# Gate loads cut in six and bound to places in the SP queue, gate stores issued from ScalarE, a shorter last norm

## The chip, the cores and the metric

One Trainium2 chip, one core in use. The metric is the device time of one execution in microseconds (us). TensorE (PE) multiplies matrices, VectorE (DVE) and ScalarE (ACT) work on tiles, GpSimd (POOL) issues indirect loads here, SyncE (SP) only issues direct loads and stores. SP, ACT and POOL each have a queue of transfers; the transfers themselves run on 16 shared DMA engines.

## The reference, cut to what matters

One decoder layer over 512 tokens of width 1024, in float32: a conditioning step, a combined projection, two kinds of attention, an output projection and a layer norm give `x1`. What the change touches is the second half, a product-key expert layer (PEER) with 16384 experts:

```
q   = h @ w_pq ; scores against sub_keys ; top 16 per half, then top 16 of the 256 pairs -> idx, g = softmax
a   = gelu(u_tab[idx] . h)
ffn = sum over idx of (g * a) * v_tab[idx]
out = LayerNorm(alpha * x1 + gate2 * ffn) * ln2_g + ln2_b
```

## The kernel before

The tokens are four tiles of 128 (`NT`). Tile 0 and half of tile 1 (`HU` = 64 tokens) fetch their experts' rows one by one, by indirect loads on POOL's queue (`fetch`, L742; one transfer brings one 1024-wide row for each of 128 partitions), followed by a DVE operation for each: a dot product with `h` (L747) for `u_tab`, an accumulation into `acc0` (L783) for `v_tab`. All other tokens are computed densely, over all experts in 128 blocks of 128.

**The u stage** (`u_block`, 128 blocks, about 345 to 970 us). A block loads 512 KB of `u_tab` (`load_raw`, L93, three buffers), splits it into a rounded part `hi` (ACT, L87) and a remainder `lo` (DVE, L88; three buffers each), multiplies with 24 matmuls of 320 columns (L97 to L99) and applies Gelu (ACT, L815). Blocks 0 to 31 keep their activations on the chip, blocks 32 to 111 store them to `a_d` from ACT's queue (L820), blocks 112 to 127 keep them again. Beside the blocks run three generators: `topk` (DVE), `make_g` and the gathers. `make_g` builds the dense gate matrix of a tile of tokens in 16 steps (one-hot vectors on DVE, scaled by eight `go` operations on ACT, 16 matmuls, two copies to `stage` on ACT); after each two steps, 1 MB goes to `g_d` in device memory, issued on SP (L700). For three tiles that is 48 steps and 24 stores. Constants set the rate per block: `GRATE` steps of `make_g`, `RA`, `RB` and `RV` us worth of gathers (each 1.25 or 1.2), and a budget of 2.6, 1.6 or 0.7 us of `topk`.

**The v stage** (`v_block` and `v_mm`, 128 blocks, about 968 to 1527 us). A block loads 512 KB of `v_tab` (L93), splits it as above, multiplies the activations with the gates to `w` (L884 on ACT, L885 on DVE), splits `w` to `wh` and `wl` (L890, L891; four buffers) and does 18 matmuls of 512 columns. The gates come in groups of eight blocks (`GB`), 16 groups, each one load of 1.5 MB in runs of 512 bytes, issued on ACT (`g_load`, L863). There are two gate buffers: `gl`, and `gl2`, which takes over the place of the transposed activations that the u stage multiplies. From the 49th block on, each block also loads its activations back from `a_d` (L881, four buffers, on SP). At block 112 seven loads of 512 KB are written down for the end (`g2r`, `ln2g`, `ln2b`, four `xr`, L912 to L917). At block 116 all gathers that are left are pulled at once, and `finish(0)` normalizes tile 0. The last six blocks are multiplied tile by tile, each followed by `finish` of that tile.

**The order.** The code is written in program order, but a planner sorts the instructions of each queue while the kernel is built: an instruction whose inputs and buffers are free by the planner's own reckoning goes ahead of one that isn't, earlier-written ones first. On the chip each queue then keeps that order strictly, so an instruction that must wait holds up all those behind it in its queue. Waits are on buffers being free, on data, and for a transfer also on an earlier transfer that used the same one of a few completion counters.

```python
nc.scalar.dma_start(gl, g_d.rearrange("g p i t -> p g (i t)")[:, :, e * TG:(e + GB) * TG])
dma(a, a_d[e - NB])
dma(g_d[(t - 1) * (P // TG) + tg], stage)
```

Of the kernel before, what the change touches and what calls it, by code (L numbers as in the profile page):

```python
# [36 lines left out]
NB = 32  # L37
GB = 8
NS = 80
GRATE = 0.54  # L40
HU = 64
T0U = P + HU
TU = S - T0U
# [1 line left out]
GBUF = 5  # L45
RA = 1.6
RB = 1.9
RV = 1.45


@with_exitstack
def layer(ctx: ExitStack, tc: tile.TileContext, A, out, dbg=None):
# [31 lines left out]
    def split(src, shape, eng_hi=None):  # L84
# [3 lines left out]
        split.last = nc.vector.tensor_sub(lo, src, hi.bitcast(F32))  # L88
        return hi, lo

    def load_raw(src, shape):
        raw = stream.tile(shape, F32, name="raw", tag="raw", bufs=3)
        dma(raw, src)  # L93
        return raw

    def mm3(ps, lh, ll, rh, rl, first, last):
        nc.tensor.matmul(ps, lh, rh, start=first, stop=False)  # L97
# [7 lines left out]
        nc.gpsimd.tensor_tensor(r, v, mhalf.to_broadcast([P, n]), op=OP.pow)  # L105
        return r

    def normalize(pool, pre, half):
        st = pool.tile([P, 2, 6], F32, name="ln_st", tag="ln_st", bufs=2)
        for i in range(2):  # L110
            half(slice(i * 512, (i + 1) * 512), i)
            nc.vector.bn_stats(st[:, i, :], pre[:, i * 512:(i + 1) * 512])
        mv = pool.tile([P, 2], F32, name="ln_mv", tag="ln_mv", bufs=2)
        nc.vector.bn_aggr(mv, st)
        r = rsqrt_eps(pool, mv[:, 1:2], 1)
        nc.vector.tensor_scalar(pre, pre, mv[:, 0:1], r, op0=OP.subtract, op1=OP.mult)

    hh = hpool.tile([P, KB, S], F32R, name="hh", tag="hh")
# [549 lines left out]
    def make_g(t, pool):  # L668
        i01, g = best[t]
        ps = accbank()  # L670
        nc.tensor.transpose(ps[:, 0:P], i01[:, 0].rearrange("p h k -> p (h k)"), ident)
        nc.tensor.transpose(ps[:, P:2 * P], i01[:, 1].rearrange("p h k -> p (h k)"), ident)
        nc.tensor.transpose(ps[:, 2 * P:3 * P], g.rearrange("p h k -> p (h k)"), ident)
        iT = pool.tile([P, 3, P], F32, name="iT", tag="iT", bufs=1)
        nc.scalar.copy(iT.rearrange("p a t -> p (a t)"), ps[:, :3 * P])
        iTb = pool.tile([P, P], BF, name="iTb", tag="iTb", bufs=1)
        nc.scalar.copy(iTb, ps[:, :P])
        for tg in range(P // TG):
            stage = pool.tile([P, NKEY, TG], F32, name="stage", tag="stage", bufs=2)
            for q in range(TG // 8):  # L680
                t0 = tg * TG + q * 8
                oh0 = pool.tile([P, P, 8], BF, name="oh0", tag="oh0", bufs=2)
                nc.vector.tensor_tensor(oh0, iTb[:, None, t0:t0 + 8].to_broadcast([P, P, 8]), iota8, op=OP.is_equal)
                oh1 = pool.tile([P, 8, P], F32, name="oh1", tag="oh1", bufs=2)
                nc.vector.tensor_tensor(oh1, iT[:, 1, t0:t0 + 8, None].to_broadcast([P, 8, P]),
                                        iota[:, None, :].to_broadcast([P, 8, P]), op=OP.is_equal)
                go = pool.tile([P, 8, P], F32, name="go", tag="go", bufs=2)
                for i in range(8):
                    nc.scalar.activation(go[:, i, :], oh0[:, :, i], AF.Copy, scale=iT[:, 2, t0 + i:t0 + i + 1])  # L689
                for u in range(2):  # L690
                    ps = accbank()
                    for i in range(4):
                        nc.tensor.matmul(ps[:, i * P:(i + 1) * P], oh1[:, 4 * u + i, :], go[:, 4 * u + i, :],  # L693
                                         start=True, stop=True)
                    w = q * 8 + u * 4
                    nc.scalar.copy(
                        stage[:, :, w:w + 4].rearrange("p i t -> p t i"), ps.rearrange("p (t i) -> p t i", t=4))
                if q < TG // 8 - 1:
                    yield
            dma(g_d[(t - 1) * (P // TG) + tg], stage)  # L700
            yield

    best = {}
# [123 lines left out]
    c1 = c2 = 0.0  # L827
    gt = gathers()
    late = []
    for e in range(NKEY):  # L830
        if e == NB + NS:
            pull(tk, 1e9)
            while not weighted:
                next(gt)
            drain(gg)
            g_stack.close()
            sel_stack.close()
            late.append(ctx.enter_context(tc.tile_pool(name="late", bufs=1, reuse_waits="tile")))
        u_block(e)
        keep(e)  # L840
        if e < NB + NS:
            budget[0] = pull(tk, budget[0] + (2.6 if 1 not in best else 1.6 if 2 not in best else 0.7))
        if 2 in best and e < NB + NS:
            c1 += GRATE
            while c1 >= 1.0:
                c1 -= 1.0
                drain(gg, 1)
        if 1 in lists:
            c2 = pull(gt, c2 + (RA if not weighted else RB))
    psB_stack.close()  # L850
    psq[:] = ctx.enter_context(tc.tile_pool(name="psC", bufs=1, space=bass.MemoryType.PSUM, reuse_waits="tile")), 2, 6

    v_stack = ExitStack()
    vp = v_stack.enter_context(tc.tile_pool(name="vp", bufs=1, reuse_waits="tile"))
    pacc = [[accbank() for _ in range(2)] for _ in range(DT)]
    order = list(range(NB)) + list(range(NB + NS, NKEY)) + list(range(NB, NB + NS))

    def g_load(e):
        if e // GB % 2 == 0:
            gl = vp.tile([P, NTG, GB * TG], F32, name="gl", tag="gl", bufs=1)  # L860
        else:
            gl = hpool.tile([P, NTG, GB * TG], F32, name="gl2", tag="hh")
        nc.scalar.dma_start(gl, g_d.rearrange("g p i t -> p g (i t)")[:, :, e * TG:(e + GB) * TG])  # L863
        return gl

    gls = {order[0]: g_load(order[0])}

    def v_block(n):
        e = order[n]
        gl = gls[e - e % GB]  # L870
        raw = load_raw(A["v_blk"][e], [P, D])
        if n < NKEY - 4:
            hi, lo = split(raw, [P, D])
        else:
            hi, lo = (b[:, n - NKEY + 4, :] for b in tail[1:])
            nc.scalar.copy(hi, raw)
            nc.vector.tensor_sub(lo, raw, hi.bitcast(F32))
        a = acts.pop(e)
        if a is None:
            a = vp.tile([P, TU], F32, name="a_b", tag="a_b", bufs=4)  # L880
            dma(a, a_d[e - NB])  # L881
        w = vp.tile([P, TD], F32, name="w", tag="w", bufs=2)
        i = e % GB
        nc.scalar.copy(w[:, 0:HU].rearrange("p (g t) -> p g t", t=TG), gl[:, 0:HU // TG, i * TG:(i + 1) * TG])  # L884
        nc.vector.tensor_mul(w[:, HU:].rearrange("p (g t) -> p g t", t=TG), a.rearrange("p (g t) -> p g t", t=TG),  # L885
                             gl[:, HU // TG:, i * TG:(i + 1) * TG])
        wp, nb = (vp, 4) if n < NKEY - 3 else (tail[0], 3)
        wh = wp.tile([P, TD], F32R, name="wh", tag="wh", bufs=nb)
        wl = wp.tile([P, TD], F32R, name="wl", tag="wl", bufs=nb)
        nc.scalar.copy(wh, w)  # L890
        pace[0], pace_next[0] = pace_next[0], nc.vector.tensor_sub(wl, w, wh.bitcast(F32))  # L891
        return n, hi, lo, wh, wl
# [8 lines left out]
    tail = [None]  # L901
    last = []
    for n in range(NKEY):
        if n % GB == 0 and n + GB < NKEY:
            gls[order[n + GB]] = g_load(order[n + GB])
        c2 = pull(gt, c2 + RV)
        if n == NKEY - 16:
            ring_stack.close()
            fin = ctx.enter_context(tc.tile_pool(name="fin", bufs=1, side="right", reuse_waits="tile"))
            tail[0] = fin  # L910
            g2r, ln2g, ln2b = (fin.tile([P, D], F32, name=nm) for nm in ("g2r", "ln2g", "ln2b"))
            dma(g2r, g2_d[0].partition_broadcast(P))  # L912
            dma(ln2g, A["ln2_g"].partition_broadcast(P))
            dma(ln2b, A["ln2_b"].partition_broadcast(P))
            xr = [fin.tile([P, D], F32, name=f"xr{t}") for t in range(NT)]
            for t in range(NT):
                dma(xr[t], x1_d[t])  # L917
            pre = [h2n] + [fin.tile([P, D], F32, name=f"pre{t}") for t in range(DT)]
            hi4 = hpool.tile([P, 4, D], F32R, name="hi4", tag="hh")
            lo4 = hpool.tile([P, 4, D], F32R, name="lo4", tag="hl")  # L920
            tail += [hi4, lo4]
        if n == NKEY - 12:
            pull(gt, 1e9)

            def finish(t, src):
# [2 lines left out]
                    nc.vector.scalar_tensor_tensor(pre[t][:, s], xr[t][:, s], ALPHA, pre[t][:, s],  # L928
                                                   op0=OP.mult, op1=OP.add)

                normalize(vp, pre[t], half)
                for f in range(2):
                    fs = slice(f * 512, (f + 1) * 512)
                    nc.vector.tensor_mul(pre[t][:, fs], pre[t][:, fs], ln2g[:, fs])
                    nc.vector.tensor_add(pre[t][:, fs], pre[t][:, fs], ln2b[:, fs])
                    dma(out[t][:, fs], pre[t][:, fs])

            finish(0, (acc0[:, 0:512], acc0[:, 512:1024]))
        blk = v_block(n)
        if n < NKEY - LAST:  # L940
            for t in range(DT):
                v_mm(t, *blk)
        else:
            last.append(blk)
# [79 lines left out]
```

## Time and profile before

| | us |
|---|---|
| median of three runs | 1546.8 (1546.06 to 1556.96) |
| the profiled execution, time | 1547.63 |
| its span in the profile | 1545.7 |
| PE busy | 1430.1 (93%) |
| DVE busy | 1265.8 (82%) |
| ACT busy | 822.6 (53%) |
| POOL busy | 462.5 (30%) |
| mean granted clock of TensorE | 0.965 |
| moved by the DMA engines | 446.17 MB, 289 GB/s |

Busy time is what an engine spends in instructions; the issue of a transfer is not counted. A count behind an x is a number of instructions. "A <- B" in a list of waits means that A stood idle until B was done.

### The profile page before, as it was taken

How to read it: one execution, taken by the hardware profiler on the slowest of the kernel's cores; microseconds unless marked ns; L12 is line 12 of the kernel's file. 1: busy time of each engine (PE TensorE's matmuls, PEld its weight loads, DVE VectorE, ACT ScalarE, POOL GpSimd, SP SyncE). 2: the span in 40 equal slices, each digit the busy share in tenths (PEclk: the TensorE clock that was granted, in tenths of full speed). 3: DMA queues.
4: the chain of work that ended last, by engine and by line, in shares of the span. 5: the costliest groups of instructions: out<-in, count | busy, mean ns of one | idle time of the engine just before them, and what ended most of it. 6: DMA issues, size and time to landing. Idle time of an engine off the chain costs nothing.

```text
span 1545.7 us, 22766 instructions
## 1 busy us (share of the span) xinstructions
PE 1430.1 (93%) x7837; PEld 1254.9 (81%) x7837; DVE 1265.8 (82%) x2606; ACT 822.6 (53%) x1523; POOL 462.5 (30%) x338
## 2 busy tenths in 40 slices
PE   6999988998789998999999969899889999999985
PEld 5677866887789998999999969788768888888854
DVE  7797675899899899678798759688679788897896
ACT  2466533334358998999798734344234343433431
POOL 0000000000344333044354436334324444454420
PEclk9999898999899999999999989999989999999997
DMA  8856363222688899699899999999989999999971
GB/s 312 286 186 196 119 203 117 84 85 67 233 282 308 314 349 332 199 339 403 347 385 380 402 322 393 337 342 321 326 304 363 370 363 374 380 356 359 374 281 54
DMA packets 180245, 446.17 MB, mean 289 GB/s; under 512 B 15329, under 2 KB 86369, under 8 KB 176930
## 3 DMA queue, kind: packets, MB, share of 16 engines
q1 hardware_dynamic: 73122, 238.66, 43.2%
q0 software_dynamic: 46080, 167.79, 28.9%
q10 hardware_dynamic: 60928, 38.28, 8.2%
q8 instruction: 61, 1.00, 0.3%
q14 instruction: 54, 0.44, 0.1%
HBM read 401.38 MB, written 43.26 MB: 288 GB/s over the span
## 4 chain that ended last, share of the span: by engine, by line
PE 49%; DVE 15%; issue 11%; DMA 9%; ACT 9%; POOL 5%; POOLq 0%; DVEq 0%; ACTq 0%; SPq 0%
PE acc L97 9%; PE acc L98 9%; PE acc L99 8%; POOL gb L742 5%; PE bank L97 5%; PE bank L98 4%; PE bank L99 4%; ACT go L689 4%; DMA gl<-g_d 4%; DVE lo L88 3%; DMA raw<-v_blk 2%; ACT hi L87 2%; PE st L98 2%; PE st L97 2%; PE st L99 2%
## 5 line engine op out<-in xcount | busy, mean ns | idle before, releaser
L87 ACT CAST hi<-raw 128x1024 fp32r<-128x1024 f32 x286 | 299.3, 1050 | 298.8 <-PE acc L99 82.6
L88 DVE TENSOR_TENSOR lo<-raw,hi 128x1024 fp32r<-128x1024 f32 x286 | 349.4, 1222 | 124.7 <-ACT hi L87 123.8
L97 PE MATMUL st<-h2h,hi 128*128 128x320 f32 x1024 | 324.1, 317 | 20.4 <-ACT hi L87 20.4
L99 PE MATMUL st<-h2h,lo 128*128 128x320 f32 x1024 | 319.7, 313 | 15.9 <-DVE lo L88 15.7
L97 PE MATMUL acc<-hi,wh 128*128 128x512 f32 x768 | 302.6, 395 | 20.0 <-ACT hi L87 13.9
L98 PE MATMUL st<-h2l,hi 128*128 128x320 f32 x1024 | 319.5, 312 | 0.0
L98 PE MATMUL acc<-lo,wh 128*128 128x512 f32 x768 | 302.2, 394 | 1.7 <-DVE lo L88 1.7
L99 PE MATMUL acc<-hi,wl 128*128 128x512 f32 x768 | 300.7, 393 | 1.1 <-DVE wl L891 1.0
L742 POOL DMA_INDIRECT gb<-v_tab,ei x128 | 182.6, 1426 | 251.4 <-DVE acc L783 228.4
L742 POOL DMA_INDIRECT gb<-u_tab,ei x128 | 179.4, 1402 | 261.2 <-DVE gb L747 192.4
L747 DVE SCALAR_TENSOR_TENSOR gb<-gb,h2n 128x1024 f32<-128x1024 f32 x192 | 231.5, 1220 | 13.0 <-DMA gb<-u_tab,ei 8.4
L97 PEld LDWEIGHTS st<-h2h,hi 128*128 128x128 f32 x1024 | 194.9, 190 | 22.3 <-ACT hi L87 22.2
L99 PEld LDWEIGHTS st<-h2h,lo 128*128 128x128 f32 x1024 | 194.3, 190 | 18.6 <-DVE lo L88 18.4
L98 PEld LDWEIGHTS st<-h2l,hi 128*128 128x128 f32 x1024 | 194.8, 190 | 0.0
L97 PEld LDWEIGHTS acc<-hi,wh 128*128 128x128 f32 x768 | 146.0, 190 | 54.4 <-ACT hi L87 15.1
L689 ACT ACTIVATE go<-oh,iT 128x128 f32<-128x128 bf16 x384 | 168.9, 525 | 8.7 <-DVE eq L649 4.9
L98 PEld LDWEIGHTS acc<-lo,wh 128*128 128x128 f32 x768 | 146.2, 190 | 33.7 <-DVE lo L88 3.4
L99 PEld LDWEIGHTS acc<-hi,wl 128*128 128x128 f32 x768 | 145.5, 190 | 33.2 <-DVE wl L891 2.7
L742 POOL DMA_INDIRECT gb<-u_tab,eip x64 | 89.9, 1405 | 264.8 <-DVE lo L88 149.7
L783 DVE SCALAR_TENSOR_TENSOR acc<-gb,w,acc 128x1024 f32<-128x1024 f32 x127 | 162.7, 1281 | 0.8 <-DMA gb<-v_tab,ei 0.6
L890 ACT CAST wh<-w 128x384 fp32r<-128x384 f32 x128 | 64.7, 511 | 117.1 <-PE acc L98 70.9
L693 PE MATMUL acc<-go,oh 128*128 128x128 f32 x768 | 108.0, 287 | 6.3 <-ACT go L689 4.1
(215 smaller groups left out, 1944.5 us busy)
## 6 DMA issues: line engine op xcount, KB each, us to landing
raw<-u_T SPq DMA_DIRECT2D x128, 512.0 KB, 6.6
raw<-v_blk SPq DMA_DIRECT2D x128, 512.0 KB, 6.7
wada<-w_adaT SPq DMA_DIRECT2D x48, 512.0 KB, 4.7
g_d<-stage SPq DMA_DIRECT2D x24, 1024.0 KB, 7.6
gl<-g_d ACTq DMA_DIRECT2D x16, 1536.0 KB, 16.5
a_d<-a_s ACTq DMA_DIRECT2D x80, 160.0 KB, 6.4
a_b<-a_d SPq DMA_DIRECT2D x80, 160.0 KB, 6.8
raw<-w_pqT SPq DMA_DIRECT2D x16, 512.0 KB, 3.6
```

Of the source, the lines that this page charges most:

```text
L87: nc.scalar.copy(hi, src)
L88: split.last = nc.vector.tensor_sub(lo, src, hi.bitcast(F32))
L97: nc.tensor.matmul(ps, lh, rh, start=first, stop=False)
L98: nc.tensor.matmul(ps, lh, rl, start=False, stop=False)
L99: nc.tensor.matmul(ps, ll, rh, start=False, stop=last)
L689: nc.scalar.activation(go[:, i, :], oh0[:, :, i], AF.Copy, scale=iT[:, 2, t0 + i:t0 + i + 1])
L693: nc.tensor.matmul(ps[:, i * P:(i + 1) * P], oh1[:, 4 * u + i, :], go[:, 4 * u + i, :], start=True, stop=True)
L742: nc.gpsimd.indirect_dma_start(out=b, out_offset=None, in_=A[tab], in_offset=bass.IndirectOffsetOnAxis(ap=idx[:, j:j + 1], axis=0))
L747: paced(nc.vector.scalar_tensor_tensor(b, b, 1.0, h2n, op0=OP.mult, op1=OP.mult, accum_out=acc))
L783: paced(nc.vector.scalar_tensor_tensor(acc0, b, w0[:, j:j + 1], acc0, op0=OP.mult, op1=OP.add))
L890: nc.scalar.copy(wh, w)
```

## The change

1. **Gate loads.** The load of a group is cut into six pieces of 256 KB (four of the 24 token groups each), issued on SP instead of ACT. Each piece is bound to stand behind the last block load written so far. For groups 1 to 15, the six pieces are written after blocks 0 to 5 of the group before; those of group 0 after u blocks 115, 117, 119, 121, 123 and 125, for which the pool of the v stage opens at block 112.
2. **Activation loads** are bound behind the block load two blocks back, **the seven end loads** behind the last block load before block 112.
3. **Gate stores** are issued on ACT.
4. **The last norm**: instead of a 1024-wide subtract-and-multiply and two operations on each half, (x - mean) * gamma and then * r + beta on each half.
5. **Rates**: `GRATE` 0.54 to 0.56, `RV` 1.45 to 1.55, the middle budget of `topk` 1.6 to 1.2.

```diff
+    def queued(ins, back=1):
+        tc.add_manual_dep(ins.ins, queue[-back].ins.name, ... NoSync ...)
+        return ins
     def load_raw(src, shape):
         raw = stream.tile(shape, F32, name="raw", tag="raw", bufs=3)
-        dma(raw, src)
+        queue.append(dma(raw, src))
...
-            dma(g_d[(t - 1) * (P // TG) + tg], stage)
+            nc.scalar.dma_start(g_d[(t - 1) * (P // TG) + tg], stage)
...
+    def g_piece(m, i):
+        e = order[m]
+        if i == 0:
+            if m // GB % 2 == 0:
+                gls[e] = vp.tile([P, NTG, GB * TG], F32, name="gl", tag="gl", bufs=1)
+            else:
+                gls[e] = hpool.tile([P, NTG, GB * TG], F32, name="gl2", tag="hh")
+        gs = slice(i * NTG // GP, (i + 1) * NTG // GP)
+        queued(dma(gls[e][:, gs], gv[:, gs, e * TG:(e + GB) * TG]))
...
         u_block(e)
+        if 0 <= e - NKEY + 2 * GP + 1 < 2 * GP and (e - NKEY) % 2:
+            g_piece(0, (e - NKEY + 2 * GP + 1) // 2)
...
-            dma(a, a_d[e - NB])
+            queued(dma(a, a_d[e - NB]), AHEAD)
...
-        if n % GB == 0 and n + GB < NKEY:
-            gls[order[n + GB]] = g_load(order[n + GB])
...
-            dma(g2r, g2_d[0].partition_broadcast(P))
+            queued(dma(g2r, g2_d[0].partition_broadcast(P)))
... (and the other six end loads)
-                    nc.vector.tensor_mul(pre[t][:, fs], pre[t][:, fs], ln2g[:, fs])
-                    nc.vector.tensor_add(pre[t][:, fs], pre[t][:, fs], ln2b[:, fs])
+                    nc.vector.scalar_tensor_tensor(pre[t][:, fs], pre[t][:, fs], mv[:, 0:1], ln2g[:, fs],
+                                                   op0=OP.subtract, op1=OP.mult)
+                    nc.vector.scalar_tensor_tensor(pre[t][:, fs], pre[t][:, fs], r, ln2b[:, fs],
+                                                   op0=OP.mult, op1=OP.add)
...
         blk = v_block(n)
+        if n % GB < GP and n - n % GB + GB < NKEY:
+            g_piece(n - n % GB + GB, n % GB)
```

`GP` is 6 and `AHEAD` is 3; `queue` collects the block loads.

## Rows read from the trace of the kernel before

**Rows 1.** Busy time (count) of each engine by stretch, granted clock, DMA share, GB/s

```profile
core 0: us, PE busy (x) PEld busy (x) DVE busy (x) ACT busy (x) POOL busy (x), PEclk, DMA share, GB/s
420.00:440.00 20.00, 14.28 (x83) 13.76 (x84) 20.00 (x44) 5.98 (x7) 10.64 (x8) 0.84 0.81 282
470.00:670.00 200.00, 192.28 (x1317) 186.76 (x1317) 172.45 (x339) 179.81 (x314) 62.36 (x45) 0.97 0.87 305
840.00:886.00 46.00, 46.00 (x335) 46.00 (x334) 36.16 (x48) 34.87 (x60) 23.36 (x17) 1.00 1.03 404
886.00:912.00 26.00, 11.74 (x65) 11.09 (x64) 8.62 (x12) 6.19 (x11) 4.54 (x4) 0.74 0.88 297
912.00:955.00 43.00, 43.00 (x295) 43.00 (x294) 40.48 (x61) 18.93 (x31) 28.76 (x20) 1.00 1.01 388
955.00:1000.00 45.00, 40.14 (x207) 34.69 (x206) 30.41 (x46) 14.85 (x23) 18.75 (x15) 0.96 0.95 351
1080.00:1130.00 50.00, 39.14 (x164) 31.14 (x163) 29.99 (x37) 14.35 (x28) 14.27 (x11) 0.89 0.89 317
1200.00:1300.00 100.00, 100.00 (x443) 82.78 (x442) 86.00 (x104) 40.86 (x74) 44.57 (x30) 1.00 1.03 370
1480.00:1517.00 37.00, 31.36 (x118) 23.58 (x119) 31.87 (x46) 12.41 (x22) 4.18 (x4) 0.91 0.51 181
1517.00:1546.00 29.00, 10.02 (x44) 7.82 (x42) 21.11 (x39) 0.00 (x0) 2.00 (x3) 0.71 0.15 55
```

**Rows 2.** Waits, 880 to 915 us: us in total, times, longest

```profile
DVE w L885 <- DMA gl<-g_d: 17.4, 1, 17.4
PE st L97 <- ACT hi L87: 11.6, 1, 11.6
ACT a_s L815 <- DMA g_d<-stage: 8.7, 1, 8.7
```

**Rows 3.** Waits of SP's queue, 880 to 960 us

```profile
SPq L93 <- DMA gl<-g_d: 10.1, 1, 10.1
SPq L881 <- DMA g_d<-stage: 6.8, 1, 6.8
```

**Rows 4.** Waits, 955 to 1005 us

```profile
ACT w L884 <- DMA gl<-g_d: 10.7, 1, 10.7
PE acc L97 <- ACT hi L87: 4.2, 1, 4.2
```

**Rows 5.** Waits, 1080 to 1135 us

```profile
PE acc L97 <- ACT hi L87: 9.6, 2, 9.4
```

**Rows 6.** Waits of SP's queue, 1080 to 1135 us

```profile
SPq L93 <- DMA gl<-g_d: 22.0, 1, 22.0
```

**Rows 7.** DMA issues by line: count, KB each, median us to landing

```profile
raw<-v_blk SPq DMA_DIRECT2D x128, 512.0 KB, 6.7
gl<-g_d ACTq DMA_DIRECT2D x16, 1536.0 KB, 16.5
xr<-x_d SPq DMA_DIRECT2D x4, 512.0 KB, 16.0
```

**Rows 8.** Waits of SP's queue, whole span

```profile
SPq L700 <- ACT go L689: 42.8, 13, 8.8
SPq L700 <- ACT stage L696: 17.5, 8, 8.6
```

**Rows 9.** ACT in order of time: start, us, instruction, idle before it

```profile
871.01 1.05 ACT L87 CAST hi<-raw 128x1024 fp32r<-128x1024 f32 x1 [0.47 <-ACT a_s L815]
```

**Rows 10.** DVE in order of time, the end

```profile
1516.87 1.29 DVE L927 TENSOR_TENSOR pre<-acc,g2r 128x512 f32<-128x512 f32 x2 [1.88 <-PE acc L99]
1536.03 0.81 DVE L116 TENSOR_SCALAR pre<-pre,ln_mv,rs_r 128x1024 f32<-128x1024 f32 x1 [0.66 <-POOL rs_r L105]
1538.09 1.29 DVE L935 TENSOR_TENSOR pre<-pre,ln2b 128x512 f32<-128x512 f32 x2
```

**Rows 11.** Line L863 on ACT's queue: ns min/median/max, first and last start

```profile
L863 ACTq EVENT_SEMAPHORE  x13: 17/200/2732, 1021.7 to 1430.2; - x13
```

More of the change, by code (lines that the diff above doesn't have):

```diff
@@ L39 @@
 NS = 80
-GRATE = 0.54
+GRATE = 0.56
 HU = 64
@@ L47 @@
 RB = 1.9
-RV = 1.45
+RV = 1.55
+GP = 6
+AHEAD = 3
 @with_exitstack
@@ L89, in split @@
         return hi, lo
+    queue = []
     def load_raw(src, shape):
         raw = stream.tile(shape, F32, name="raw", tag="raw", bufs=3)
-        dma(raw, src)
+        queue.append(dma(raw, src))
         return raw
+    def queued(ins, back=1):
+        tc.add_manual_dep(ins.ins, queue[-back].ins.name,
+                          mybir.DependencyInfo(mybir.DependencyClass.NoSync, mybir.DependencyReason.DATA),
+                          reason="behind the block's load")
+        return ins
     def mm3(ps, lh, ll, rh, rl, first, last):
@@ L106, in rsqrt_eps, with normalize @@
         return r
-    def normalize(pool, pre, half):
+    def normalize(pool, pre, half, raw=False):
         st = pool.tile([P, 2, 6], F32, name="ln_st", tag="ln_st", bufs=2)
@@ L115, in normalize @@
         r = rsqrt_eps(pool, mv[:, 1:2], 1)
+        if raw:
+            return mv, r
         nc.vector.tensor_scalar(pre, pre, mv[:, 0:1], r, op0=OP.subtract, op1=OP.mult)
@@ L829, in layer @@
     late = []
+    order = list(range(NB)) + list(range(NB + NS, NKEY)) + list(range(NB, NB + NS))
+    v_stack = ExitStack()
+    gls = {}
+    gv = g_d.rearrange("g p i t -> p g (i t)")
+    def g_piece(m, i):
[7 more added lines that the diff above has]
+        queued(dma(gls[e][:, gs], gv[:, gs, e * TG:(e + GB) * TG]))
     for e in range(NKEY):
@@ L838, in layer @@
             late.append(ctx.enter_context(tc.tile_pool(name="late", bufs=1, reuse_waits="tile")))
+            vp = v_stack.enter_context(tc.tile_pool(name="vp", bufs=1, reuse_waits="tile"))
         u_block(e)
+        if 0 <= e - NKEY + 2 * GP + 1 < 2 * GP and (e - NKEY) % 2:
+            g_piece(0, (e - NKEY + 2 * GP + 1) // 2)
         keep(e)
         if e < NB + NS:
-            budget[0] = pull(tk, budget[0] + (2.6 if 1 not in best else 1.6 if 2 not in best else 0.7))
+            budget[0] = pull(tk, budget[0] + (2.6 if 1 not in best else 1.2 if 2 not in best else 0.7))
         if 2 in best and e < NB + NS:
@@ L851, in layer @@
     psq[:] = ctx.enter_context(tc.tile_pool(name="psC", bufs=1, space=bass.MemoryType.PSUM, reuse_waits="tile")), 2, 6
-    v_stack = ExitStack()
-    vp = v_stack.enter_context(tc.tile_pool(name="vp", bufs=1, reuse_waits="tile"))
     pacc = [[accbank() for _ in range(2)] for _ in range(DT)]
[L856 to L866, printed above, removed]
     def v_block(n):
@@ L911, in layer @@
             g2r, ln2g, ln2b = (fin.tile([P, D], F32, name=nm) for nm in ("g2r", "ln2g", "ln2b"))
-            dma(g2r, g2_d[0].partition_broadcast(P))
-            dma(ln2g, A["ln2_g"].partition_broadcast(P))
-            dma(ln2b, A["ln2_b"].partition_broadcast(P))
+            queued(dma(g2r, g2_d[0].partition_broadcast(P)))
+            queued(dma(ln2g, A["ln2_g"].partition_broadcast(P)))
+            queued(dma(ln2b, A["ln2_b"].partition_broadcast(P)))
             xr = [fin.tile([P, D], F32, name=f"xr{t}") for t in range(NT)]
             for t in range(NT):
-                dma(xr[t], x1_d[t])
+                queued(dma(xr[t], x1_d[t]))
             pre = [h2n] + [fin.tile([P, D], F32, name=f"pre{t}") for t in range(DT)]
@@ L929, in half @@
                                                    op0=OP.mult, op1=OP.add)
-                normalize(vp, pre[t], half)
+                mv, r = normalize(vp, pre[t], half, raw=True)
                 for f in range(2):
                     fs = slice(f * 512, (f + 1) * 512)
-                    nc.vector.tensor_mul(pre[t][:, fs], pre[t][:, fs], ln2g[:, fs])
-                    nc.vector.tensor_add(pre[t][:, fs], pre[t][:, fs], ln2b[:, fs])
+                    nc.vector.scalar_tensor_tensor(pre[t][:, fs], pre[t][:, fs], mv[:, 0:1], ln2g[:, fs],
+                                                   op0=OP.subtract, op1=OP.mult)
+                    nc.vector.scalar_tensor_tensor(pre[t][:, fs], pre[t][:, fs], r, ln2b[:, fs],
+                                                   op0=OP.mult, op1=OP.add)
                     dma(out[t][:, fs], pre[t][:, fs])
```

## The prediction

> **What bounds the kernel now.** I read the busy time by stretch first, then the waits inside the stretches where TensorE stands idle, then SP's queue there, then the end. TensorE is the bound wherever nothing stalls it: it is busy for all of 840 to 886, 912 to 955 and 1200 to 1300 us [rows 1]. These stretches give its price per matmul: 46/335 = 0.137 us with gate building beside it, 43/295 = 0.146 us for u blocks alone, 100/443 = 0.226 us for v blocks, so 18 x 0.226 = 4.06 us for a v block and 24 x 0.146 = 3.5 us for a u block. Against those prices the other stretches show what is lost:
>
> - 886 to 912: 65 x 0.146 = 9.5 us of work in 26 us, **16.5 lost**, 14.3 of it idle and the rest at a lower granted clock (0.74).
> - 955 to 1000: 45 - 40.1 = **4.9** idle.
> - 1080 to 1130: 164 x 0.226 = 37.0 in 50, **13.0 lost**.
> - 470 to 670: 1317 x 0.137 = 181 in 200, **19 lost**.
> - 1480 to 1517: 118 x 0.226 = 26.6 in 37, **10.4 lost**; and from 1517 on 19 us without a matmul.
>
> The first three have one cause. After 880 VectorE comes to the product `w` of the first v block, which the planner had put far ahead, and waits 17.4 us for group 0's gates [rows 2]; no `lo` and no dot product can pass. ACT stands 8.7 us at the issue of that gate load, because the last gate store into the same place hasn't landed, and Gelu waits behind it; TensorE then lacks `hi` for 11.6 us [rows 2]. SP does the same twice: four activation loads for block 48 and on stand 6.8 us in front of the u loads, and the next u load then waits 10.1 us for the gate load, with which it shares no data, so by a shared completion counter [rows 3]. After 955 ACT waits 10.7 us for group 1 [rows 4]. After 1080 the seven end loads, which the planner put some 80 blocks early, and a gate load run together; SP's next block load waits 22.0 us for that gate load [rows 6], and TensorE 9.6 us for `hi` [rows 5].
>
> **The change, part by part.**
>
> *Group 0.* The pieces now stand behind the loads of u blocks 115 to 125, on SP, so nothing on ACT waits for the last store, and `w` of block 0 can't be planned before the sixth piece. I credit the 16.5 us and take back two things. The 1.5 MB move into a stretch that already runs at 388 GB/s [rows 1]: 4 us at that rate if TensorE has to wait for all of it, 0 if the lead of three buffers covers it. And `w` may still be planned a little too early: at worst the landing of a piece, for which a block load is the nearest row, 6.7 us [rows 7]. I take 5.5 back, as the stretch is nearly full: **-11** (-16.5 to -6).
>
> *Group 1* still can't start before the u stage ends, since it takes the place of the u stage's operand. It needs to be there 8 x 4.06 = 32 us later; before, it was missed only by a product planned early. Six pieces in line with the block loads should land sooner: **-4** (-4.9 to 0).
>
> *1080 to 1130.* Both ingredients go: **-13**. But the seven end loads, 3.67 MB, come back behind block load 111. They were 16.0 us in landing [rows 7]. Block load 112 stands behind them. A block load is issued three blocks (12 us) ahead and normally lands in 6.7, and the split leads the matmuls by some two more blocks, so a delay of 10 to 16 us eats the lead and a little more: **+4** (0 to 13, the last if the collision simply moves).
>
> *Gate stores on ACT.* On SP they stood 42.8 + 17.5 us waiting for ACT [rows 8], with block loads behind them, in the stretch that lost 19 us. On ACT, the copies they wait for are just in front. What that gives lies between 0 and -13, the part of the 19 us that 60 us of waits could explain; what it costs is 24 issues of up to 0.47 us, as that of an activation store, which let ACT stand that long before its next cast [rows 9]: 0 to +11, on an engine already busy 180 of 200 us there. Nearest the middle of both: -6 + 3 = **-3**. The rule for moving a transfer between queues speaks against more: by the Trainium skill ("DMA: Bandwidth & Descriptors", section "Issuing engines are not separate DMA queues") all queues share the same DMA engines and a move saves only issue time; by that alone this term would be 0 instead of -3. The rows show the other thing at stake, waiting in line on the issuing engine.
>
> *topk budget and GRATE.* VectorE is busy 20 of 20 us at 420 to 440 while TensorE idles 5.7 [rows 1]. A quarter less topk per block there defers work to where VectorE has room: **-2** (-5 to +2). The 48 steps still end near block 106 (adding up the rates), so nothing is left for block 112.
>
> *RV.* Per v block 1.55/1.2 = 1.29 gathers instead of 1.21; adding up the costs, 16 instead of 19 are left at block 116. Three of about 1.2 us less on VectorE in the stretch that lost 10.4: -2 (-4 to 0). On the way VectorE goes from 86 to about 88 of 100 us: covered by TensorE. The transfers get 3% more: +1 (see the first rival). Together **-1**.
>
> *Last norm.* From 1516.87 to 1539.4 VectorE works almost without a pause [rows 10], while the matmuls end at about 1527. Three tiles each lose one operation of 0.81 us, spaced 0.74, and the wait for POOL's root (0.66 in the last) now lies beside the first of the new pair: **-3** (-0.7 to -3.5). The new operations replace as many 512-wide ones, which I price alike.
>
> *At nothing:* 80 more issues on SP. SP spends most of its time waiting for `lo`, which covers them; bare, they'd be 80 x 0.4 = 32 us of SP alone.
>
> Sum: -11 - 4 - 13 + 4 - 3 - 2 - 1 - 3 = **-33**. The profiled execution took 1547.6 (span 1545.7), 0.8 above the median of the runs: 1547.6 - 33 = 1514.6, on the scale of the median **1514**.
>
> **The rivals.**
>
> *Transfers become the bound of the v stage.* From block 48 a block moves 524 KB of `v_tab`, 164 of activations, 197 of gates and 1.29 x 524 of gathers: 1.56 MB, at 4.06 us 384 GB/s. The stretch 1200 to 1300 shows 370 at a full DMA share [rows 1]. If that is the ceiling for this mix, a block takes 4.22 us, 80 blocks +13: about **1527**. Against it: 404 and 388 GB/s in two other stretches, and no idle TensorE at 370. The Trainium skill (same page, "Specifications") gives a limit of about 358 GB/s of device memory per core; as an estimate that would be 4.36 us per block and +24; the 404 GB/s of 840 to 886 disagree with it for a core that runs alone. Chance 0.13.
>
> *The end loads' collision just moves,* +13 instead of +4, and part of the u stall stays because `w` is still planned too early, -6 instead of -11: about **1528**. Chance 0.10.
>
> *The bindings don't cure the early planning:* the planner puts `w` of block 0 or the pieces where VectorE waits as now, and only 1080 to 1130 and the norm are gained: -13 + 4 - 3 - 2 = about **1533**. Chance 0.10.
>
> *Slower: SP stands on gate buffers.* A piece that comes up in SP's order before its buffer is free stops all block loads behind it. Decisive is whether the last `w` of the group before is done when the first piece is reached. If it is late by enough to cost one block (4.06 us) in each of 14 groups, that is +57: about **1571**. Against it: the same wait on ACT's queue had a median of 0.2 us and at most 2.7 [rows 11], so the buffer was nearly free where the load stood. Chance 0.08.
>
> The forecast keeps 0.59, with its own range of 1503 to 1526.
>
> **The numbers.** Predicted 1514. The range of 8 in 10 takes in the forecast with the favourable ends of the store and u-stall terms (1499) and the first three rivals (to 1538); outside are the slower rival and some extremes. About 1% (15 us) can be told from no change: faster than 1531 holds for the forecast and the first two rivals, less their upper tails: 0.79. Within 1% the third rival and those tails: 0.13. Slower: 0.08.
>
> **What would show it.** Right: TensorE busy through what was 886 to 912; no `w` on VectorE waiting over 5 us for gates; pieces landing in under 12 us; SP's block loads never behind a gate load for 10 us; some 3 us less after the last matmul. A new short gap near block 112. Wrong: v blocks above 4.1 us with `hi` waiting for block loads (first rival), or SP's pieces waiting for `w` with TensorE short of `hi` every eighth block (last rival). The prediction fails if the new order of the u stage costs more than its -5, which no row can exclude.

## The result, and the profile after

The kernel after takes **1559.8 us** (median of 20 runs, 1553.55 to 1564.62) against 1546.66 for before (20 runs), a ratio of **1.0076** [1.0057, 1.0094]: 12 to 13 us slower, where 33 less was predicted. The profiled execution took 1554.1 us (span 1552.3), at the low end of its runs. Every view below shows one such execution, and those of one kernel can lie 10 us apart, so times are compared by their medians and views by the work done in a stretch.

Busy time by stretch, kernel after, in the columns of [rows 1]:

```profile
470.00:670.00 200.00, 183.80 (x1255) 178.70 (x1254) 163.94 (x334) 171.11 (x298) 57.76 (x37) 0.97 0.79 278
886.00:912.00 26.00, 25.93 (x181) 25.66 (x180) 19.40 (x26) 12.61 (x18) 14.44 (x10) 1.00 1.01 394
912.00:955.00 43.00, 36.39 (x229) 35.72 (x228) 28.31 (x41) 12.20 (x19) 24.22 (x17) 0.88 0.93 344
955.00:1000.00 45.00, 40.92 (x226) 36.97 (x225) 37.71 (x58) 17.78 (x33) 23.99 (x18) 0.96 0.96 342
1080.00:1130.00 50.00, 50.00 (x222) 41.44 (x221) 43.50 (x58) 19.71 (x37) 24.32 (x16) 1.00 0.99 349
1400.00:1480.00 80.00, 72.84 (x307) 58.57 (x306) 61.23 (x71) 27.87 (x48) 35.54 (x23) 0.96 1.03 381
470.00:840.00 370.00, 346.62 (x2384) 337.44 (x2383) 292.06 (x499) 322.80 (x568) 126.17 (x84) 0.97 0.85 306
1200.00:1400.00 200.00, 197.34 (x861) 160.47 (x860) 170.92 (x205) 80.28 (x144) 108.07 (x62) 1.00 1.02 370
```

Two stretches of the kernel before that [rows 1] doesn't have:

```profile
470.00:840.00 370.00, 361.69 (x2529) 354.19 (x2529) 314.69 (x525) 333.44 (x592) 140.22 (x99) 0.99 0.91 336
1400.00:1480.00 80.00, 78.59 (x343) 63.65 (x341) 67.79 (x78) 31.09 (x53) 34.33 (x28) 1.00 1.02 373
```

What was to go has gone in two places: 886 to 912 is full, and 1080 to 1130 holds 222 matmuls instead of 164. But the stall at the end of the u stage has moved on to 912 to 955 (229 matmuls, 33.4 us of work at 0.146, so 9.6 of 43 lost), 1400 to 1480 has a new gap, and 470 to 670, where nothing was to get worse, has 62 matmuls fewer than in [rows 1]. From 470 to 840 it is 2384 against 2529: 145 matmuls, 20 to 21 us at the prediction's prices for the u stage (0.137 and 0.146). A smaller loss is easily passed over: 1200 to 1400 has 861 where TensorE in before was busy throughout and did 884, 23 x 0.226 = 5.2 us.

The waits tell where. Waits of the kernel after from 405 to 960 us (us in total, times, longest), three of the lines on Gelu (`a_s`), `w` and `st`:

```profile
ACT a_s L827 <- PE st L109: 29.4, 31, 2.7
PE st L107 <- ACT hi L89: 25.3, 16, 6.3
...
ACT w L900 <- DMA gl<-g_d: 14.3, 1, 14.3
```

The first two in the kernel before, same stretch:

```profile
ACT a_s L815 <- PE st L99: 5.8, 1, 5.8
PE st L97 <- ACT hi L87: 18.9, 5, 11.6
```

Before, Gelu waited once for `st` (5.8 us); now 31 times, 29.4 us in all, and TensorE waits for casts 16 times instead of 5 (25.3 us against 18.9, of which the stall of [rows 2] is 11.6). One such place shows how it works. First ScalarE in order of time (start, length, instruction, idle before it and its releaser), kernel after:

```profile
690.85 1.76 ACT L701 ACTIVATE go<-oh,iT 128x128 f32<-128x128 bf16 x4
692.52 1.89 ACT L708 COPY stage<-acc 128x512 f32<-128x512 f32 x2
694.21 1.99 ACT L89 CAST hi<-raw 128x1024 fp32r<-128x1024 f32 x2
...
701.53 0.44 ACT L827 ACTIVATE a_s<-st 128x320 f32<-128x320 f32 x1 [0.19 <-PE st L109]
701.86 1.04 ACT L89 CAST hi<-raw 128x1024 fp32r<-128x1024 f32 x1
```

then TensorE in the same microseconds, kernel after:

```profile
690.91 2.24 PE L705 MATMUL acc<-go,oh 128*128 128x128 f32 x10 [0.27 <-ACT go L701]
695.31 0.41 PE L107 MATMUL st<-h2h,hi 128*128 128x320 f32 x1 [2.16 <-ACT hi L89]
696.25 0.63 PE L107 MATMUL st<-h2h,hi 128*128 128x320 f32 x1 [0.38 <-ACT hi L89]
```

and by stretch, kernel after:

```profile
680.00:690.00 10.00, 9.61 (x65) 9.12 (x65) 5.89 (x10) 7.70 (x16) 2.65 (x3) 1.00 0.69 240
695.30:699.50 4.20, 3.81 (x14) 3.55 (x15) 2.35 (x2) 4.20 (x10) 0.00 (x0) 0.59 1.00 376
699.50:704.00 4.50, 4.50 (x33) 4.50 (x32) 2.99 (x3) 4.31 (x9) 0.00 (x0) 1.00 0.67 182
```

The cast that TensorE needs stands behind four `go` and two copies to `stage`, and TensorE idles 2.16 us for it. After that pause the mean granted clock is 0.59 for 4.2 us, near the lower of its two levels (1.2 GHz): 14 matmuls where the next 4.5 us hold 33. At 701.53 the opposite: Gelu comes up before its matmuls are done and the next cast waits behind it, here for 0.19 us only (the longest of the 31 is 2.7). ScalarE works with next to no lead over TensorE.

The rest answers to the prediction's other steps. ScalarE around the end of the u stage, kernel after:

```profile
909.92 0.33 ACTq L832 DMA_DIRECT2D a_d<-a_s  x1
924.16 0.39 ACT L900 COPY w<-gl 128x64 f32<-128x64 f32 x2 [14.27 <-DMA gl<-g_d]
924.46 1.04 ACT L89 CAST hi<-raw 128x1024 fp32r<-128x1024 f32 x1
```

These are the copies `w` of v blocks 0 and 1. They read token groups 0 to 3, which are the first piece and nothing of the others, so the planner could put them behind piece 0, in front of the casts of the last u blocks. Piece 0 was issued at 911.78 and landed 12.4 us later, a little over the 12 us that the prediction allowed for a piece. SP at the end loads, and what ScalarE sees of it, kernel after (in order of time; the issues of `ln2g` and `ln2b`, between the second and the third line, are left out):

```profile
1434.06 0.33 SPq L97 DMA_DIRECT2D raw<-v_blk  x1
1434.44 0.70 SPq L926 DMA_DIRECT2D g2r<-g_d  x1
1436.47 4.04 SPq L931 DMA_DIRECT2D xr<-x_d  x4
1442.82 0.33 SPq L97 DMA_DIRECT2D raw<-v_blk  x1
```

```profile
1457.11 1.04 ACT L89 CAST hi<-raw 128x1024 fp32r<-128x1024 f32 x1 [12.71 <-DMA raw<-v_blk]
```

The block load behind the seven was issued 8.8 us after the one ahead of them and the cast waited 12.7 us. The line of the four `xr` runs from the start of the first issue to the end of the last; one issue takes 0.32 us. The end, VectorE in order of time, kernel after:

```profile
1541.49 1.40 DVE L948 SCALAR_TENSOR_TENSOR pre<-pre,ln_mv,ln2g 128x512 f32<-128x512 f32 x2
1542.82 1.41 DVE L950 SCALAR_TENSOR_TENSOR pre<-pre,rs_r,ln2b 128x512 f32<-128x512 f32 x2
```

TensorE's last matmul began at 1536.03 (before: 1526.63), with 1552.3 - 1536.0 = 16.3 us to the end of the span against 19.1: 2.8 us saved.

### The profile page after: what moved, and what is told of

Read it like the earlier page. It is cut to its first block, busy times and chain, and to the rows that moved or that the text cites. A ratio compares the mean times of both kernels' runs of the same rounds, so it can differ in the third digit from the quotient of the medians.

```text
span 1552.3 us, 22791 instructions
## 1 busy us (share of the span) xinstructions
PE 1436.5 (93%) x7837; PEld 1257.6 (81%) x7837; DVE 1264.1 (81%) x2602; ACT 826.3 (53%) x1523; POOL 509.7 (33%) x338
## 3 DMA queue, kind: packets, MB, share of 16 engines
q0 software_dynamic: 46080, 167.79, 28.8%
## 4 chain that ended last, share of the span: by engine, by line
PE 35%; issue 29%; POOL 17%; DVE 9%; DMA 5%; ACT 4%; SPq 0%; POOLq 0%; DVEq 0%; ACTq 0%
POOL gb L754 16%; PE bank L107 4%; PE bank L109 4%; PE bank L108 4%; PE acc L107 4%; PE acc L108 4%; PE acc L109 4%; PE st L109 2%; PE st L107 2%; PE st L108 2%; DVE lo L90 2%; DMA raw<-w_k 1%; PE acc L705 1%; PE bank L377 1%; ACT hi L89 1%
## 5 line engine op out<-in xcount | busy, mean ns | idle before, releaser
L107 PE MATMUL st<-h2h,hi 128*128 128x320 f32 x1024 | 330.1, 322 | 27.0 <-ACT hi L89 26.9
L109 PE MATMUL st<-h2h,lo 128*128 128x320 f32 x1024 | 324.4, 319 | 16.6 <-DVE lo L90 16.4
L108 PE MATMUL st<-h2l,hi 128*128 128x320 f32 x1024 | 324.3, 317 | 0.0
L754 POOL DMA_INDIRECT gb<-u_tab,ei x128 | 190.4, 1488 | 276.2 <-DVE gb L759 181.9
L754 POOL DMA_INDIRECT gb<-v_tab,ei x128 | 212.2, 1658 | 205.2 <-DVE acc L795 189.4
L759 DVE SCALAR_TENSOR_TENSOR gb<-gb,h2n 128x1024 f32<-128x1024 f32 x192 | 230.2, 1218 | 15.8 <-DMA gb<-u_tab,ei 11.6
L107 PEld LDWEIGHTS st<-h2h,hi 128*128 128x128 f32 x1024 | 199.0, 194 | 31.9 <-ACT hi L89 31.7
L108 PEld LDWEIGHTS st<-h2l,hi 128*128 128x128 f32 x1024 | 199.1, 194 | 0.0
L754 POOL DMA_INDIRECT gb<-u_tab,eip x64 | 95.5, 1492 | 257.7 <-DVE tv L566 149.5
L108 PEld LDWEIGHTS acc<-lo,wh 128*128 128x128 f32 x768 | 145.3, 189 | 42.4 <-DVE lo L90 12.1
L701 ACT ACTIVATE go<-oh,iT 128x128 f32<-128x128 bf16 x384 | 173.9, 518 | 2.0 <-DVE oh L695 1.4
L900 ACT COPY w<-gl 128x64 f32<-128x64 f32 x128 | 31.0, 243 | 176.8 <-DVE wl L907 159.8
```

The lines of the kernel that those rows point to most:

```text
L108: nc.tensor.matmul(ps, lh, rl, start=False, stop=False)
L109: nc.tensor.matmul(ps, ll, rh, start=False, stop=last)
L754: nc.gpsimd.indirect_dma_start(out=b, out_offset=None, in_=A[tab], in_offset=bass.IndirectOffsetOnAxis(ap=idx[:, j:j + 1], axis=0))
L759: paced(nc.vector.scalar_tensor_tensor(b, b, 1.0, h2n, op0=OP.mult, op1=OP.mult, accum_out=acc))
```

## The experiments

Each run is compared with runs of before on the same chip. The first theory was that the stores on ScalarE cost the time and the pieces are fine; the rivals were the rates, `w` planned early, and the end loads.

**u1_store_sp.** The stores back on SP, all else as after.

```diff
-            nc.scalar.dma_start(g_d[(t - 1) * (P // TG) + tg], stage)
+            dma(g_d[(t - 1) * (P // TG) + tg], stage)
```

> The changed kernel with the 24 gate stores back on SP's queue, all else as changed. Theory A (the stores' issues on ACT put Gelu and the casts of the u stage into a worse planned order, and the 18 us that the u stage lost at 470 to 840 us come from that): 15 to 22 us faster than the changed kernel, ACT's wait for st in the a_s rows falls from 29 us to under 10. Theory B (the changed rates do it): the same time within 5 us, the wait stays. Theory C (neither, the loss is the pieces' doing): the same time.

Measured: 1533.89 us, 0.9917 [0.989, 0.9944]: 26 us less than after, by one line, and more than the 15 to 22 that theory A gave. The wait of `a_s` for `st` is gone from the list, `w` on ScalarE still waits (u1_store_sp, waits from 405 to 960):

```profile
ACT w L900 <- DMA gl<-g_d: 12.2, 1, 12.2
PE st L107 <- ACT hi L89: 11.4, 4, 5.7
```

A yardstick for the u stage is the time from the first to the last Gelu of blocks 32 to 111. Line `a_s` by instruction (ns min/median/max, first and last start), kernel after, then u1_store_sp:

```profile
L827 ACT ACTIVATE a_s<-st x80: 409/437/478, 517.1 to 925.4; 128x320 f32<-128x320 f32 x80
```

```profile
L827 ACT ACTIVATE a_s<-st x80: 409/430/494, 519.9 to 902.9; 128x320 f32<-128x320 f32 x80
```

408.3 us against 383.0.

**u2_rates.** `GRATE`, `RV` and the middle budget of `topk` as before.

```diff
-GRATE = 0.56
+GRATE = 0.54
-RV = 1.55
+RV = 1.45
...
-... 1.2 if 2 not in best else 0.7))
+... 1.6 if 2 not in best else 0.7))
```

> The changed kernel with the three rates of before (0.54, 1.45, 1.6), stores still on ACT. Theory A: within 5 us of the changed kernel, the wait of Gelu for st stays near 29 us. Theory B: 15 to 22 us faster, and 540 to 700 us no longer lose matmuls.

Measured: 1557.56 us, 1.0078 [1.0043, 1.0113], which can't be told from after; Gelu still waits for `st` 23 times, 27.3 us. The rates aren't the loss. That they do nothing does not follow: 1200 to 1400 is full again (kernel u2_rates),

```profile
1200.00:1400.00 200.00, 200.00 (x884) 165.68 (x883) 169.26 (x205) 81.92 (x146) 103.05 (x59) 1.00 1.02 368
```

which is 5.2 us more work there than in after, while the first Gelu of block 32 comes 5.5 us later (522.6 against 517.1). Two effects may cancel; the second one is no larger than the spread of that start among kernels with the same rates (512.8 to 523.1).

**c1_w_late.** `w` of v blocks 0 and 1 bound behind the last u block's Gelu (ScalarE) and remainder (VectorE).

```diff
+        if n < 2:
+            behind(cw, gelus[-1])
+            behind(mw, los[-1])
```

> The changed kernel with one thing more: the copy (ACT) and the product (DVE) that make w of v blocks 0 and 1 are bound behind the Gelu and the split of the last u block. Theory: the u stage's end loses some 10 us because ACT stands 14.3 us at a copy that needs only the first piece of group 0, and DVE 4.9 us at a product; bound later, both waits go and the kernel is 8 to 12 us faster than the changed one. Rival (the first v blocks then start late): the gap moves to the first v blocks and nothing or less than 3 us is gained.

Measured: 1548.68 us, 0.9998 [0.9969, 1.0027], 11 less than after; first to last Gelu takes 399.0 us (520.5 to 919.5), 9.3 less. So the copy's wait is worth about 10 us, as its theory had it, and is apart from the loss further up: here Gelu still waits 28.8 us for `st`. (The profiled execution, 1556.54 us, is the slowest of its ten; the 11 us are from the medians.)

**c2_end_spread.** The seven end loads one in every second v block from 33 to 45, instead of all behind block load 111.

```diff
-        if n == NKEY - 16:
+        if n == NB + 1:
...
+        if n > NB and (n - NB) % 2 and (n - NB) // 2 < 7:
+            queued(dma(*ends[(n - NB) // 2]))
```

> The changed kernel with the seven end loads written one every second block from v block 33 to 45 instead of together at block 112. Theory: the burst behind block load 111 delays the next block load so that ACT waits 12.7 us and TensorE loses about 8 us at 1440 to 1460; spread where no activation loads run, that goes: 6 to 9 us faster than the changed kernel. Rival (the transfers are full there anyway, and a delay comes back elsewhere): under 3 us.

Measured: 1560.3 us, 1.0086 [1.0053, 1.0119]: nothing gained, as the rival had it. The gap itself is cured; the stretch of the burst, kernel c2_end_spread:

```profile
1400.00:1480.00 80.00, 78.71 (x346) 64.52 (x345) 72.63 (x85) 31.37 (x56) 43.02 (x28) 1.00 1.04 378
```

346 matmuls instead of 307 (8.8 us at 0.226), but the time stayed: 1000 to 1400 has 1696 instead of 1729 (7.5 us less work), and over the whole run the casts waited 77.8 us for v rows against 42.0 in after. What is gained behind 1400 is lost ahead of it, where the loads are now. These stretches had a DMA share of about 1.0 already; that this is the reason was not tried by itself.

**b1_store_act.** The other way round: before, with the one line of u1 reversed, so that only the stores move to ScalarE.

> The kernel before with one edit: the 24 gate stores issued on ACT. Theory A (either form): the wait of Gelu for st appears here too (20 to 30 us), and the u stage from block 32 to 111 takes 15 to 25 us longer; the kernel is 12 to 25 us slower than before. Rival (the store's move hurts only together with the pieces): within 5 us of before.

Measured: 1562.89 us, 1.0109 [1.0056, 1.0161], 16 us slower than before. First to last Gelu 407.0 us (526.9 to 933.9) against 381.3 in before (532.3 to 913.6), 26 us more; why 10 of them are not in the time was not followed. Gelu's wait is about that of after (kernel b1_store_act, waits from 405 to 960):

```profile
ACT a_s L815 <- PE st L99: 29.3, 25, 4.8
```

So the stores alone make the new wait. Not by their issue, however. The stores' line, kernel after:

```profile
L712 ACTq DMA_DIRECT2D g_d<-stage x24: 326/326/348, 477.8 to 893.0; - x24
L712 ACTq EVENT_SEMAPHORE  x2: 17/17/17, 527.7 to 647.2; - x2
```

24 x 0.326 = 7.8 us of issue and no wait worth the name. Two theories were left: the planner, which puts ScalarE's other instructions in another order once the stores are among them, or a cost on the chip that the rows do not show (the transfers on another queue, the issues at a bad moment). In the built programs the order does differ: when ScalarE comes to the Gelu of a block, it has cast `hi` on average 2.5 blocks beyond that block in before and in u1_store_sp, 1.7 in after and in b1_store_act (blocks 32 to 111; counted along ScalarE's instructions in the traces, no times).

**c3_cast_first.** Gelu of block e bound behind the cast of block e + 3, stores still on ScalarE.

```diff
+        if e >= NB + 3 and e - 3 < NB + NS:
+            tc.add_manual_dep(gelus[e - 3].ins, split.cast.ins.name, ... NoSync ...)
```

> The changed kernel, stores still on ACT, with one edit: the Gelu of u blocks 32 to 111 is bound behind the cast hi of the block three further on, the order that most blocks of the kernel before have. Theory A1 (the stores cost time by the order that the planner makes on ACT: Gelu ahead of the next casts): 15 to 25 us faster than the changed kernel, the wait of a_s for st under 8 us. Theory A2 (they cost time on the chip, by 24 issues on ACT or by a third busy queue): less than 5 us faster.

Measured: 1549.33 us, 1.0009 [0.9985, 1.0033]: 10 of the 26 us; first to last Gelu 395.9 us (520.6 to 916.5). The wait of `a_s` for `st` is gone, but ScalarE now stands at another place, and TensorE waits for `lo` and `hi` (c3_cast_first, waits from 405 to 960):

```profile
ACT stage L709 <- PE acc L706: 19.2, 17, 3.1
PE st L110 <- DVE lo L90: 18.2, 15, 3.2
PE st L108 <- ACT hi L89: 15.6, 8, 6.1
```

Half an answer: repairing one pair of the order pushed the wait to the next pair. The cast is now three blocks ahead at each of the 80 Gelus, more than the 2.5 of before, so its lead is not all that the order changes. The run doesn't tell the theories apart for the other 16.

**c4_act_sp_order and c5_sp_act_order** do. The built order of ScalarE's, VectorE's and TensorE's instructions in the stretch where they differ (713, 353 and 1576 of them) was read from one kernel and forced on the other, each instruction bound behind the one ahead of it. c4 has the stores on ScalarE with the order of u1_store_sp, c5 the stores on SP with the order of after; the places of the transfers are not forced. In the traces c4 and u1, and c5 and after, agree in every instruction of the three engines over the whole run (1523, 2602 and 7837).

```diff
+    for plan in PLAN:
...
+        for one, two in zip(line, line[1:]):
+            tc.add_manual_dep(two, one.name, ... NoSync ...)
```

> The kernel after with its gate stores still on ScalarE's queue, but with ScalarE's, VectorE's and TensorE's own instructions of the u stage held in the order that they have in u1_store_sp (stores on SyncE); nothing else is changed. Theory A, that the stores' place costs by the order that the planner makes of the other instructions: the time of u1_store_sp, 0.992 of before, about 1534 us, and the wait of the Gelu for TensorE's st falls from 29 us to under 8. Rival B, that the 24 issues themselves on ScalarE, or the transfers on a third queue, cost the time: it stays where c3_cast_first was or the kernel after, 1.001 to 1.008 of before, 1548 to 1559 us, and ScalarE shows waits behind its issues. A value between, 0.996, would share it out.

> The other half of that square: the kernel u1_store_sp, gate stores on SyncE's queue, with the three engines' instructions of the u stage held in the order that they have in the kernel after. Theory A (the order costs): as slow as the kernel after, 1.006 to 1.01 of before, 1556 to 1562 us, with the Gelu's wait for st back at 25 us or more, although no store is issued on ScalarE. Rival B (the issues or the queue cost): as fast as u1_store_sp, 0.99 to 0.994, about 1534 us.

Measured, with the first to last Gelu in brackets:

| | order of u1_store_sp | order of after |
|---|---|---|
| stores on SP | u1: 0.9917 [0.989, 0.9944] (383.0 us) | c5: **1.0084** [1.0054, 1.0114] (411.5 us) |
| stores on ScalarE | c4: **0.9903** [0.9871, 0.9935] (385.5 us) | after: 1.0076 [1.0057, 1.0094] (408.3 us) |

The time goes with the order, 26 to 27 us in either row (0.0167 and 0.0173 of 1547), and not with the queue: in either column the two differ by less than their intervals. The stores' line in c4_act_sp_order, then its waits from 405 to 960, then those of c5_sp_act_order:

```profile
L768 ACTq DMA_DIRECT2D g_d<-stage x24: 326/326/347, 482.4 to 876.3; - x24
```

```profile
ACT w L956 <- DMA gl<-g_d: 13.7, 1, 13.7
PE st L165 <- DVE lo L146: 13.6, 8, 4.6
PE st L163 <- ACT hi L145: 8.8, 4, 6.0
```

```profile
ACT a_s L886 <- PE st L168: 30.1, 31, 2.5
PE st L166 <- ACT hi L148: 22.8, 16, 6.6
```

c4 issues its 24 stores from ScalarE at 0.326 us each like after, and Gelu's wait for `st` does not appear in its list at all; c5 issues none there and has it back, 31 times as in after. Theory A holds in both runs. What the two don't separate is which of the three engines' orders matters, and which places in it.

**v1_sp_late** puts together what helped: stores on SP and `w` late.

> The changed kernel with both edits that helped: stores back on SP, and w of v blocks 0 and 1 bound behind the last u block. If the two losses are separate, they add: 26 + 11 us faster than the changed kernel, about 1522 to 1526, 1.5% faster than before. If they share a cause, about 1533, as with the stores alone.

Measured: 1528.7 us, 0.9893 [0.9843, 0.9944], between the two expectations, and the interval covers both. In the u stage the losses do add: first to last Gelu 372.6 us (519.1 to 891.7) is 35.7 less than after, against 25.3 in u1 and 9.3 in c1. That the medians of v1 and u1 are only 5 us apart was not followed; the two profiles can't say (u1's execution took 1540.7 us, the slowest of six, v1's 1523.25, the fastest of four). What is left to gain lies near the end: 268 matmuls in 1400 to 1480 are 60.6 of 80 us at 0.226.

**v2_rv_spread** is v1 with `RV` at 1.45 and the end loads spread as in c2.

> v1 with RV back at 1.45 and the seven end loads spread over v blocks 33 to 45. Theory (the transfers bound the v stage at 1.29 gathers per block, and the burst at block 112 costs 8 us): 1200 to 1400 us holds 880 matmuls or more instead of some 850, and the kernel is 8 to 16 us faster than v1. Rival (what the v stage gains comes back at block 116, where 19 instead of 16 gathers are left): less than 4 us faster than v1.

Measured: 1526.64 us, 0.9883 [0.9833, 0.9933]: not to be told from v1. 1200 to 1400 holds 862 matmuls (v1: 871), not 880, so the theory missed, and the time fits the rival.

**v3_xr_late** and **v4_xr_late_rv**: v1 with three of the end loads in blocks 119 to 121, where the gathers are over, and the same with `RV` at 1.45.

```diff
+        if 0 <= n - NKEY + 9 < DT:
+            t = n - NKEY + 10
+            queued(dma(xr[t], x1_d[t]))
```

> v1_sp_late with the residual rows of token tiles 1 to 3 (three of the seven end loads, 1.5 MB) loaded in v blocks 119 to 121, where the gathers' transfers have ended, and not in the burst at block 112. Theory: the burst delays the v rows because the transfers are full there; with 1.5 of its 3.5 MB gone to a stretch with idle transfer engines, the cast's longest wait for the v rows (13.2 us in v1) falls under 9 and the end comes 3 to 5 us earlier: 0.986 of before, about 1524 us. Rival: TensorE lags there because of VectorE's dots and products of the gathers, and the time stays at 0.989, with the wait gone or not.

> v3_xr_late with the gathers of the v stage paced as in before, 1.45 us in a block and not 1.55. The prediction gave the faster pace a gain of 1 us because the gathers end earlier; theory: they already run as fast as the transfers allow, so that the pace moves the time by under 2 us either way, 0.985 to 0.988. Rival: the faster pace crowds the v rows' loads in full transfers, and v4 is 3 us or more faster than v3.

Measured: v3 **1525.55** us, 0.987 [0.9832, 0.9909], the best here, 20 less than before; v4 1531.91 us, 0.9909 [0.9874, 0.9943]. The longest wait for a v row fell as expected (ScalarE's waits from 1400 to 1480, v1_sp_late, then v3_xr_late):

```profile
ACT hi L89 <- DMA raw<-v_blk: 23.5, 7, 13.2
```

```profile
ACT hi L89 <- DMA raw<-v_blk: 24.8, 7, 8.1
```

but the sum of the waits did not, so the burst was cut in pieces more than removed, and that stretch has 275 matmuls against 268. v4 missed both expectations: the slower pace of the gathers came out 6 us slower, not equal or faster. In the two profiles v4 does 19 matmuls more than v3 in 1200 to 1400 (878 against 859) and 29 fewer in 1400 to 1480 (246 against 275): what the slower pace saves on the way is lost again where the gathers that are left come together. The intervals of v1 to v4 overlap; which of them is best stays open, that all four beat before doesn't.

## Why the prediction was wrong

**Gate stores on ACT, -3 (range -13 to +11): the step that failed.** Measured: +16 alone in before, +26 in the company of the other parts. The prediction looked for the gain and the cost at the moved instruction: 60 us of waits on SP [rows 8], up to 0.47 us per issue on ScalarE [rows 9]. Both were read rightly and are nearly worthless. The waits on SP were covered: u1 keeps the stores on SP, where they still wait 51.5 us for ScalarE (41.4 and 10.1), and is the faster kernel. The issues took 0.326 us each, 7.8 us of an engine that, in the right order, has room for them (c4). The Trainium skill ("DMA: Bandwidth & Descriptors", section "Issuing engines are not separate DMA queues") holds that starting transfers from several engines saves only the time that it takes to start them; c4 against u1, 0.9903 and 0.9917 with overlapping intervals, agrees with it for the move by itself, and its 0 would have been the better term there. What neither contained is the order of the other instructions, which the square of c4 and c5 shows to be worth 26 to 27 us. The prediction saw that it can't be excluded ("if the new order of the u stage costs more than its -5, which no row can exclude"), and left it without a price, a term and a chance. What could have been read before: ScalarE is busy 180 of 200 us and TensorE 192 [rows 1], so neither has time to catch up on the other, and a change of ScalarE's list is one at the bound. A bound was to be had too: a cast of 1.05 us [rows 9] that is no longer covered, in each of 80 blocks, is 84 us; the 26 lie within it and far beyond the +11 that was allowed. Why the planner, once it has 24 short issues more on ScalarE, puts the casts 0.8 blocks later, and what else in the order costs time (c3), was not followed.

**Group 0, -11: mis-sized.** The gap of 16.5 us became one of 9.6, a gain of 7, at the small end of the range. The prediction bound the pieces and reasoned on VectorE's product, which needs the last piece, and indeed no product waits over 5 us. It overlooked that ScalarE's copy needs the first one only. c1 and v1 show the rest of the gap to be worth 9 to 10 us of the u stage.

**Group 1, -4:** TensorE idles 4.1 instead of 4.9 [rows 1], about -1. VectorE still comes early to a product there, kernel after, 955 to 1005:

```profile
DVE w L901 <- DMA gl<-g_d: 4.9, 1, 4.9
```

**1080 to 1130, -13:** right. 222 - 164 = 58 matmuls at 0.226 are 13.1 us.

**End loads, +4 (0 to 13):** +8; 1400 to 1480 has 307 matmuls where before had 343, 36 x 0.226. The lead was eaten as described. Spreading the loads brings nothing (c2).

**Rates, -3:** 0 by u2, within some 5 us. In the term for `RV`, the +1 for fuller transfers was too small. In 1200 to 1400 the kernels before, b1 and u2 (all three with 1.45) do 884 matmuls and the nine kernels with 1.55 do 847 to 873, so the faster pace most likely costs 5 us there in after (2 to 8 in the nine). (v2 and v4, with 1.45 and stores and `w` as in v1, have 862 and 878.) This is the sign that the prediction gave for its first rival: a v block takes 200 x 18 / 861 = 4.18 us, above 4.1, and the casts wait for block loads 18 times, 12.1 us, against 2 times, 2.5 us, in before. The rival's price was 13 us; about 5 shows in these 200 us. What the faster pace gains at the end (v3 against v4) may pay for it. Block 32 begins 15 us earlier (517.1 against 532.3), but 5.5 at most is the rates' own (u2: 522.6).

**Last norm, -3:** 2.8 in after, and the same in u1 and c4 (16.3 us from the last matmul's start to the end), but 1.0 in the one profile of u2 (18.0 us): within the range. The pair's operations are a little dearer than the old ones, 1.40 against 1.29 us for two, which the prediction had priced alike.

**SP issues, 0, and SP standing on gate buffers:** right that it doesn't decide. No block load waits for `gl` any more, and by far the largest of SP's waits is for the remainders `lo`. Activation loads come later now and VectorE waits for them 29 times, 39.8 us, 21 of these in 1200 to 1400, where before has no such wait. By themselves they cost TensorE nothing there: u2 has 20 of them, 27.6 us, and its full 884 matmuls.

Summed: without the stores -30 was predicted and -13 measured (u1). Of these 17 us, with the sizes found in after, 4 are group 0, 3 group 1, 4 the end loads and 3 the rates; 3 are not accounted for. The stores' step is 29 us off in the kernel after, and 29 + 14 = 43 of the 46 between 1514 and 1559.8.

## What to carry to other kernels

Where a planner sorts the instructions of each queue, a transfer moved to an engine has two costs: its own issue there, and the new order of all the rest; the second has to be read from the built order of the two programs. Here, on an engine that feeds the bound with little lead, it was the larger one: 26 us against 7.8 us of issues. To tell the two apart, force one program's order on the other: here that settled in two runs what a single repaired pair (c3) had left half open. And when a load is cut into pieces, look for the reader that needs only the first of them: it is now free to be put early, and it is that one that will stand and wait.

## What the runs showed of the hardware

A pause of TensorE can cost more than its length, and two of nearly the same length differed in this. In the kernel after, 2.16 us idle up to 695.31 were followed by 4.2 us at a mean granted clock of 0.59; 2.11 us idle up to 578.25 were followed by 4.2 us at 1.00 with 30 matmuls (kernel after):

```profile
578.20:582.40 4.20, 4.15 (x30) 4.15 (x31) 4.20 (x7) 3.54 (x8) 2.49 (x2) 1.00 0.63 147
```

The 24 transfers of 1 MB ran as well from ScalarE's queue as from SP's, with the order of the rest held the same (1534.57 against 1533.89 us). An issue took about the same on either engine: 0.326 us for a store of 1 MB on ScalarE, 0.33 for a block load and 0.32 for a load of `xr` on SP.
